# Decoder block on one core: the recurrent branch's output projection as seven block products under the attention, with its operands, weights and block differences prepared in other places

## The chip, the cores and the metric

The kernel runs on 1 core of a Trainium2 chip. The metric is the device time of one execution in microseconds (us). A TensorE (PE) matmul writes PSUM, a memory of eight banks of 128 x 512 fp32; VectorE (DVE), ScalarE (ACT) and GpSimd (POOL) work element by element, and SyncE (SP) issues most of the DMA transfers. Each engine works through its own queue in order.

## The reference

```python
h = rms_norm(x, g_norm) * (1 + scale) + shift            # x: 2048 x 1024
x_rnn, z_rnn, q, k, v, z_attn, g_r, g_a = split(h @ w_in)
xc = causal_depthwise_conv(x_rnn, conv_w, conv_b)
hr = rg_lru(xc, ...)                                      # a scan over the positions
y_rnn = (hr * silu(z_rnn)) @ w_out_rnn                    # 1024 x 1024: what the change touches
o = dilated_attention_mixture(rope(q), rope(k), v)
y_attn = (o * silu(z_attn)) @ w_out_attn
merged = sigmoid(g_r + b_r) * y_rnn + sigmoid(g_a + b_a) * y_attn
out = rms_norm(x + gate * (merged @ w_o), g_final)
```

## The kernel before

Every product is made in near-fp32: an operand is split into a high part and a low part (high = the value rounded to the matmul's format, low = the rest), and `mm3` (L154) issues three matmuls, high x high, high x low, low x high. What is called a product below is 12 such matmuls: a 128 x 512 block of weights against a 512 x 512 block of data, which fills one PSUM bank.

The kernel has three stages. In the **first**, run twice (f = 0, 1, one half of the 2048 positions each), `h @ w_in` is made by `strassen` (L355): two 128-column tiles of weights are a pair, and a pair is done in 7 products in place of 8, by block sums of both operands. A half has 28 pairs, that is 196 products. The order is written out by hand: `recurrent` (L928) is one pair per row tile m of the recurrent branch, followed by `others[m]` pairs of the other columns (others = 1, 2, 2, 1, 2, 2, 1, 3), so that the tiles m of a half start at products 0, 14, 35, 56, 70, 91, 112 and 126. Convolution, gates and scan of tile m are steps at fixed numbers of products after its pair (`steps_after`, L236), and the branch's result goes to a DRAM tensor `yaT`. In the second half the split weight sums of the first half come back from DRAM (`sD`, a ring of seven tiles S0 to S6, L319), one transfer of 512 KB per product. There, too, `output_weights` (L428) prepares the weights of the later projections: every 4 products a 128 x 512 half tile is loaded, split (ACT the high part, POOL the low part) and stored to `wD` in two transfers by ACT's queue; those of the attention's projection are stored unsplit to `wR` as well.

In the **second** stage the attention runs: 16 heads' halves of 6 units each, one unit per slot. In a slot PE makes scores, turns probabilities (`pT`) and sums values; DVE and ACT do the softmax and split the turned probabilities. Between these pieces lies the *fill*: `spend` (L1862) takes `FILL` steps per slot from the generator `steps` (L1731), 2.85 per slot in the first half of the heads and 2.75 in the second. A step is one `mm3` of 512 columns. The steps are those of the two output projections, in tiles of 8 steps (1024 rows of weights against 512 positions); a tile fills one PSUM bank, of which the pool `pj` has two here, and DVE multiplies it by the gate (`evict`, L1792), one step after the next tile's start. Under the attention lie `TAIL0` = 40 tiles: the recurrent branch's 32 (4 blocks of positions by 8 row tiles) and the attention's first 8. Weights come from `wD` one half tile at a time into a ring of four (L342), asked for three half tiles ahead; data tiles of `yaT` are split into high and low parts on DVE, ACT and POOL (L1771).

The **third** stage is the rest of the attention's projection and `w_o`.

Of the kernel before, what the change touches and what calls it, by code (L numbers as in the profile page):

```python
# [20 lines left out]
P = 128  # L21
# [13 lines left out]
FILL = (2.85, 2.75)  # L35
# [55 lines left out]
def decoder_block(ctx, tc, x, c, positions, g_norm, w_mod, b_mod, w_in, b_gate, conv_w, conv_b,  # L91
# [31 lines left out]
    wD = scratch("wD", [2, KT, 2, P, 2, KH, P])  # L123
# [195 lines left out]
    def load_next():  # L319
# [6 lines left out]
        elif n >= 28 * 7:  # L326
# [3 lines left out]
            if k < 3:  # L330
                load_wd(0, 0, k) if k < 2 else load_wd(0, 1, 0)
            if k == 1:

                t = T(hp, [P, KH, CH], F32, "T", bufs=14)
                nc.sync.dma_start(t[:], yaT[KH * P :, :CH].rearrange("(k p) j -> p k j", p=P))
                for i in range(KH):
                    Y0[True, 0, KH + i] = t[:, i, :]
# [4 lines left out]
    def load_wd(i, m, half):  # L342
        x = n_w[0]
        n_w[0] += 1
        W[x] = t = T(pS, [P, 2, KH, P], F32R, f"S{x % 4}")
        nc.sync.dma_start(t[:].bitcast(F32), wD[i, m, half])
# [81 lines left out]
    def output_weights():  # L428

        parts = [(i, w, m, half) for i, w in enumerate((w_out_rnn, w_out_attn)) for m in range(KT) for half in range(2)]  # L430
        for x, (i, w, m, half) in enumerate(parts):
            v = {}

            def load(v=v, w=w, m=m, half=half):
                v["raw"] = raw_tile([P, KH, P])
                rows = slice(half * KH * P, (half + 1) * KH * P)
                nc.sync.dma_start(v["raw"][:], w[0, rows, m * P : (m + 1) * P].rearrange("(k p) m -> p k m", p=P))

            def split(v=v):
                v["h"] = T(wq, [P, KH, P], F32R, "s1", bufs=1)  # L440
                v["l"] = T(wq, [P, KH, P], F32R, "s2", bufs=1)
                hi_act(v["h"][:], v["raw"][:])
                lo_pool(v["l"][:], v["raw"][:], v["h"][:])

            def store(v=v, i=i, m=m, half=half):
                for l, n in enumerate("hl"):
                    nc.scalar.dma_start(wD[i, m, half, :, l], v[n][:].bitcast(F32))
# [4 lines left out]
            for d, fn in ((1, load), (3, store_raw), (4, split), (5, store)) if i else ((1, load), (4, split), (5, store)):  # L452
                after_prod.setdefault(n_prod[0] + 4 * x + d, []).append(fn)
# [586 lines left out]

    def rotary_tables(rp, f):
# [287 lines left out]
    for f in range(2):  # L1329
# [21 lines left out]
        for m in range(KT):  # L1351
            recurrent(rp, bigr, f, m)
# [36 lines left out]
    NY = 9  # L1389
# [337 lines left out]
    TAIL0 = KT * (NB + 1)  # L1727
    RAW = 2 * TAIL0 + 1


# [501 lines left out]
```

## Time and profile before

| | |
|---|---|
| median of 3 runs | 2160.72 us (2160.36 to 2161.0) |
| the profiled execution's own time | 2161.23 us |
| its span, first to last instruction | 2159.4 us, granted clock 0.998 |
| first stage, second half (about 800 to 1340) | PE without a gap between 800 and 1200 |
| second stage (about 1345 to 1870) | PE busy 519.34 of 525 us, DVE 380.96, ACT 401.49, POOL 311.36 |
| third stage (2000 to 2160) | PE busy 151.63 of 160 us, DVE 121.95, ACT 57.96, POOL 83.27 |

A group's row gives busy time and the mean ns of one instruction. Matmul records overlap: one of 512 columns is shown with about 390 ns, but they follow each other more closely, so their cost is read from how many a stretch holds.

### The profile page before, as it was taken

The numbers are of one execution on the slowest core, as the hardware profiler recorded it, in microseconds if no ns is written. First come the engines' busy times: TensorE is split into PE (matmuls) and PEld (weight loads), VectorE is DVE, ScalarE is ACT, GpSimd is POOL, SyncE is SP. The second block draws the span as 40 slices with busy tenths as digits, with TensorE's granted clock in tenths as the row PEclk, the third lists the DMA queues.
The fourth block names the chain that finished last, engine by engine and source line by source line (L and its number), as shares of the span: only waits on it lengthen the run. The fifth ranks groups of instructions, "written<-read, shape, count | busy, mean of one in ns | idle before, by whom it ended". The sixth has DMA issues, their size and how long they took to land.

```text
span 2159.4 us, 32571 instructions
## 1 busy us (share of the span) xinstructions
PE 2136.6 (99%) x10539; PEld 1788.3 (83%) x10539; DVE 1463.3 (68%) x2582; ACT 1296.2 (60%) x2592; POOL 1120.6 (52%) x868
## 2 busy tenths in 40 slices
PE   9999999999999999999999999999999999999998
PEld 6888778888888888888888887889898988878887
DVE  6759878768656715544436684587777687788777
ACT  5748668668644527457457532677788888443333
POOL 1467667777666423223223675466666664432555
PEclk9999999999999999999999999999999999999999
DMA  8467887887655368899997676888887777899543
GB/s 301 142 211 256 280 290 264 288 294 244 174 115 166 108 229 291 301 305 311 323 318 240 152 173 171 300 269 263 273 275 218 256 236 239 300 316 300 181 170 114
DMA packets 416575, 521.39 MB, mean 241 GB/s; under 512 B 107574, under 2 KB 282898, under 8 KB 415380
## 3 DMA queue, kind: packets, MB, share of 16 engines
q1 hardware_dynamic: 376388, 401.65, 59.7%
q10 hardware_dynamic: 34384, 99.78, 12.2%
q0 software_dynamic: 5632, 17.88, 2.6%
q8 instruction: 83, 1.36, 0.3%
q14 instruction: 88, 0.72, 0.1%
HBM read 332.02 MB, written 187.17 MB: 240 GB/s over the span
## 4 chain that ended last, share of the span: by engine, by line
PE 71%; DVE 4%; DMA 3%; issue 1%; POOL 1%; ACT 1%; SPq 0%; ACTq 0%; POOLq 0%; DVEq 0%
PE X L152 14%; PE V L152 13%; PE pj L152 12%; PE Z L152 7%; PE W L152 7%; PE Y L152 6%; PE sc L152 4%; PE o L152 4%; PE pg L152 1%; PE pT L1568 1%; PE pT L1581 1%; DMA fg<-gaT 1%; DMA kraw<-kqT 1%; DVE ptl L169 1%; DVE yl L169 1%
## 5 line engine op out<-in xcount | busy, mean ns | idle before, releaser
L166 POOL TENSOR_TENSOR S<-R,S 128x512 fp32r<-128x512 f32 x192 | 295.3, 1546 | 169.3 <-ACT S L160 82.9
L152 PE MATMUL V<-T,S 128*128 128x512 f32 x1344 | 324.3, 390 | 1.9 <-DVE ev L461 1.9
L152 PE MATMUL X<-T,S 128*128 128x512 f32 x1344 | 323.8, 390 | 1.6 <-ACT u L391 1.3
L152 PE MATMUL pj<-yh,S 128*128 128x512 f32 x896 | 321.6, 402 | 1.3 <-DVE fg L1795 0.8
L152 PEld LDWEIGHTS X<-T,S 128*128 128x128 f32 x1344 | 251.8, 188 | 56.5 <-ACT u L391 2.9
L152 PEld LDWEIGHTS V<-T,S 128*128 128x128 f32 x1344 | 251.9, 188 | 55.9 <-issue 1.9
L166 POOL TENSOR_TENSOR S<-s,S 128x512 fp32r<-128x512 f32 x116 | 173.3, 1494 | 150.1 <-ACT S L160 114.3
L152 PEld LDWEIGHTS pj<-yh,S 128*128 128x128 f32 x896 | 168.3, 188 | 32.3 <-DVE S L169 1.3
L1481 ACT ACTIVATE pp<-pp,st 128x256 f32<-128x256 f32 (+3 forms) x256 | 133.8, 524 | 78.0 <-DVE st L1480 77.4
L152 PE MATMUL pj<-yl,S 128*128 128x512 f32 x448 | 175.5, 392 | 1.0 <-POOL yl L166 1.0
L160 ACT ACTIVATE S<-s 128x512 fp32r<-128x512 f32 x124 | 77.3, 624 | 145.1 <-DVE s L291 92.1
L152 PE MATMUL W<-T,S 128*128 128x512 f32 x672 | 161.6, 389 | 0.0
L152 PE MATMUL Y<-T,S 128*128 128x512 f32 x672 | 161.6, 389 | 0.0
L152 PE MATMUL Z<-T,S 128*128 128x512 f32 x672 | 161.4, 389 | 0.0
L160 ACT ACTIVATE S<-R 128x512 fp32r<-128x512 f32 x200 | 121.5, 622 | 59.0 <-DMA R<-in_w_in_dram 14.8
L169 DVE TENSOR_TENSOR ptl<-pT,pth 128x384 fp32r<-128x384 f32 (+1 forms) x160 | 97.8, 628 | 80.5 <-ACT pth L160 78.4
L152 PEld LDWEIGHTS W<-T,S 128*128 128x128 f32 x672 | 126.0, 188 | 26.9 <-issue 0.9
L152 PEld LDWEIGHTS Z<-T,S 128*128 128x128 f32 x672 | 126.2, 188 | 26.2
L152 PEld LDWEIGHTS Y<-T,S 128*128 128x128 f32 x672 | 126.1, 188 | 26.1
L166 POOL TENSOR_TENSOR s<-R,s 128x512 fp32r<-128x512 f32 x32 | 43.2, 1350 | 188.8 <-ACT s L160 164.6
L980 DVE SCALAR_TENSOR_TENSOR xc<-xr,par,xc 128x512 f32<-128x512 f32 x96 | 102.0, 1062 | 52.1 <-ACT xc L974 49.9
L1548 ACT ACTIVATE pp<-pp,M 128x256 f32<-128x256 f32 (+3 forms) x256 | 118.0, 523 | 12.8 <-DVE M L1680 12.8
(419 smaller groups left out, 4906.0 us busy)
## 6 DMA issues: line engine op xcount, KB each, us to landing
sD<-S ACTq DMA_DIRECT2D x140, 512.0 KB, 3.7
S<-sD SPq DMA_DIRECT2D x140, 512.0 KB, 5.0
S<-wD SPq DMA_DIRECT2D x82, 512.0 KB, 5.5
R<-in_w_in_dram SPq DMA_DIRECT2D x144, 256.0 KB, 3.3
wD<-s ACTq DMA_DIRECT2D x64, 256.0 KB, 5.1
kraw<-kqT SPq DMA_DIRECT2D x32, 384.0 KB, 5.1
T<-in_w_mod_dram SPq DMA_DIRECT2D x16, 512.0 KB, 9.1
vN<-ev SPq DMA_DIRECT2D x32, 256.0 KB, 2.7
```

What stands on the lines that cost most here:

```text
L152: nc.tensor.matmul(o, lhsT=l, rhs=r, start=st, stop=sp, **kw)
L160: nc.scalar.activation(o, i, AF.Copy)
L166: nc.gpsimd.tensor_tensor(o, i, h.bitcast(F32), ALU.subtract)
L169: return nc.vector.tensor_tensor(o, i, h.bitcast(F32), ALU.subtract).ins
L980: nc.vector.scalar_tensor_tensor(xc, xr[:, i : i + CH], cw(i), xc, ALU.mult, ALU.add)
L1481: nc.scalar.activation(pdst, pdst, AF.Exp, bias=m_, scale=-1.0, accum_out=l_)
L1548: nc.scalar.activation(pp, pp, AF.Copy, scale=w)
L1568: nc.tensor.transpose(pt[:, c0 + j * P : c0 + (j + 1) * P], pp[i][:, k * P : (k + 1) * P], ident)
L1581: nc.tensor.transpose(pt[:, c * P : (c + 1) * P], pp[:, half * P : (half + 1) * P], ident)
```

## The change

The recurrent branch's projection is cut into 2 x 2 blocks of 512: for each of two pairs of position blocks (q) and each of four pairs of row tiles (p), seven products give what eight gave, as the first stage does. Seven kinds of data block (`BLOCKS`: two parts of `yaT` as B11, B21, then the sums T2, T3, T1, T4, and B22) times two q are the 14 groups g of the new loop; in a group the same four data tiles serve four products, one per p. A product is 4 steps in one bank of `pj` in place of 8, so the fill has 224 steps for this projection where it had 256, and `FILL` is 2.54 and 2.44. The pool `pj` still has two banks.

What goes with it:
- Weights: `output_weights` loads four quarter blocks per p, makes four sums on DVE and splits and stores seven tiles (`wB`), one every 3 products; the attention's half tiles follow every 3 products in place of 4, four of them between p = 1 and p = 2.
- Data sums: `block_sums` loads four 128 x 512 tiles of `yaT`, makes four differences on POOL and stores them to `tB`, all issued by SP. Six of its eight calls run in the second half of the first stage, in the buffers of the recurrence (gi, y, a, t or xc, xh, xl) between two of its uses, at products 24 to 30 after the start of m = 1, 2, 4 and 5 and at 19 to 25 after that of m = 5 and 7; two run at the start of the attention.
- In the fill, data tiles are loaded straight into one of eight pairs of operand tiles (F0 to F13 and S3) during the first steps of the group before, and split there: high part on ACT for half of the first seven groups and on DVE otherwise, low part on POOL. Weights have a ring of three tiles and are asked for two tiles ahead.
- Eviction (`block_evict`): a copy (B11), one addition (T2, T3), two operations (B21, T4, B22) or three (T1).

The core of the diff:

```diff
-FILL = (2.85, 2.75)
+FILL = (2.54, 2.44)
...
+    def load_w_tile(src, ring=4):
...
+    BLOCKS = (("B11", 0), ("B21", 4), ("T2", 1), ("T3", 2), ("T1", 3), ("T4", 5), ("B22", 6))
+    N_WB = 2 * 7 * KH
+
+    def load_wb(x):
+        load_w_tile(wB[BLOCKS[x // KH % 7][1], x % KH], 3)
...
     def output_weights():
...
+        n0, PITCH = n_prod[0], 3
...
+            on_n(n, split)
+            on_n(n + 1, store)
...
+            for x, (i, name, *sums) in enumerate((
+                (5, "a22"), (3, "a22", "a21", "a22", ALU.add), (0, "a11"), (1, "a22", "a22", "a11", ALU.subtract),
+                (2, "a21", "a11", "a21", ALU.subtract), (4, "a12"), (6, "a12", "a12", "a22", ALU.subtract))):
...
+    def block_sums(q, k, on_step, tiles):
...
+        def combine(dst, a, b):
+            nc.gpsimd.tensor_tensor(raws[dst].bitcast(F32), raws[a].bitcast(F32), raws[b].bitcast(F32), ALU.subtract)
+
+        def store(i, src):
+            nc.sync.dma_start(tB[q, i, k], raws[src].bitcast(F32))
+
+        for d, fn, *args in ((0, load, *B11), (0, load, *B12), (0, load, *B22), (1, load, *B21),
+                             (3, combine, B11, B12, B11), (3, combine, B12, B22, B12), (4, combine, B22, B22, B11),
+                             (4, store, 0, B11), (4, store, 2, B12), (5, combine, B21, B21, B22), (5, store, 1, B22),
+                             (6, store, 3, B21)):
...
-    TAIL0 = KT * (NB + 1)
+    NT = 1
+    TAIL0 = KT * NT
...
+        def block_evict(g, p, ps):
+            name = BLOCKS[g % 7][0]
+            tt = nc.vector.tensor_tensor
+            if name == "B11":
+                U[p] = T(fl, [P, CH], F32, f"F{14 + p}")
+                nc.vector.tensor_copy(U[p][:], ps[:])
+            elif name in ("T2", "T1"):
+                tt(U[p][:], ps[:], U[p][:], ALU.add)
+            elif name == "T3":
+                Q[p] = T(pR, [P, CH], F32, f"R{p}")
+                tt(Q[p][:], ps[:], U[p][:], ALU.add)
+            if name in OUT:
+                t = G[g, p]
+                tt(ps[:], ps[:], (Q if OUT[name][0] else U)[p][:], ALU.add)
+                tt(t[:], ps[:], t[:], ALU.mult)
...
+        for g in range(14):
+            for p in range(KH):
+                ps = T(pj, [P, CH], F32, "pj")
+                x = KH * g + p
+                for k in range(KH):
+                    j, n = KH * p + k, KH * (g + 1)
+                    if k == 1:
+                        if x:
+                            (load_wb(x + 2) if x + 2 < N_WB else load_w(x + 2 - N_WB))
...
+                        if last:
+                            block_evict(*last)
...
+                    w, (yh, yl) = W[x], OT[KH * g + k]
+                    mm3(ps[:], w[:, 0, k, :], w[:, 1, k, :], yh[:], yl[:], first=k == 0, last=k == KH - 1)
...
+                    if j < KH and n + j > 6:
+                        operand(n + j)
+                    if j >= 8 and j % 2 == 0 and n + j // 2 - 4 > 6:
+                        split(n + j // 2 - 4)
```

The change also alters what stands where. DVE's queue at the start of the attention, before: kq are the first head's queries and keys (L169 makes their low parts, which wait for a load and for ACT), pj the fill's banks, sc the scores, pp the softmax.

```order
L169 TENSOR_TENSOR kq_2215_12040<-kraw_2235_12086,kq_2215_12040 128x512
L169 TENSOR_TENSOR kq_2215_12040<-kraw_2236_12088,kq_2215_12040 128x512
L1795 TENSOR_TENSOR fg_2232_12073<-pj_2233_12077,fg_2232_12073 128x512
L169 TENSOR_TENSOR kq_2215_12040<-kraw_2238_12092,kq_2215_12040 128x512
L1442 CAST q1_2244_12148<-kq_2215_12040 128x512 x2
L1480 ISA pp_2247_12159,st_2245_12151<-sc_2246_12152,msk_2214_12038 128x128
L1480 ISA st_2245_12151 128x1
L1480 ISA pp_2247_12159,st_2245_12151<-sc_2246_12152,msk_2214_12038 128x256
L1480 ISA st_2245_12151 128x1
L1795 TENSOR_TENSOR fg_2242_12133<-pj_2240_12118,fg_2242_12133 128x512
```

The same place now (F14 to F17 are the sums U of the four p):

```order
L1934 COPY F14_2286_12284<-pj_2278_12255 128x512
L171 TENSOR_TENSOR kq_2263_12224<-kraw_2279_12262,kq_2263_12224 128x512
L171 TENSOR_TENSOR kq_2263_12224<-kraw_2280_12264,kq_2263_12224 128x512
L1934 COPY F15_2289_12305<-pj_2284_12278 128x512
L171 TENSOR_TENSOR kq_2263_12224<-kraw_2282_12268,kq_2263_12224 128x512
L1516 CAST q1_2291_12322<-kq_2263_12224 128x512 x2
L1554 ISA pp_2294_12333,st_2292_12325<-sc_2293_12326,msk_2262_12222 128x128
L1554 ISA st_2292_12325 128x1
L1554 ISA pp_2294_12333,st_2292_12325<-sc_2293_12326,msk_2262_12222 128x256
L1554 ISA st_2292_12325 128x1
L1934 COPY F16_2297_12344<-pj_2287_12299 128x512
L1911 TENSOR_REDUCE S3_2283_12276<-S3_2283_12276 128x512
```

Four steps fill a bank now, so between the same pieces of the attention stand three evictions in place of two; the second and the third still come behind the low parts of kq.

SP's queue in the second half of the first stage, around product 112, before (each S<-sD is one product's weights; ev and zs are results on their way out):

```order
L324 DMA S6_1850_9988<-sD 128x1024
L324 DMA S0_1851_9990<-sD 128x1024
L437 DMA R3_1852_9995<-in_w_out_attn_dram 128x4x128
L324 DMA S1_1855_10012<-sD 128x1024
L1188 DMA kqT<-ev_1846_9951 384x1x128
L1188 DMA kqT<-ev_1846_9951 128x1x128
L324 DMA S2_1859_10036<-sD 128x1024
```

The same place now:

```order
L326 DMA S6_1880_10105<-sD 128x1024
L326 DMA S0_1881_10107<-sD 128x1024
L1091 DMA tB<-xc_1864_10012 128x512
L1091 DMA tB<-xc_1865_10014 128x512
L326 DMA S1_1886_10132<-sD 128x1024
L1260 DMA kqT<-ev_1877_10067 384x1x128
L1260 DMA kqT<-ev_1877_10067 128x1x128
L1085 DMA gi_1887_10141<-yaT 128x512
L1085 DMA y_1888_10143<-yaT 128x512
L1085 DMA a_1889_10145<-yaT 128x512
L1091 DMA tB<-xh_1866_10016 128x512
L326 DMA S2_1893_10166<-sD 128x1024
```

Between the same weights SP now issues three stores of differences, which wait for POOL, and three loads of the next call.

204 lines of the change are left out of this document (155 added, 49 removed).

## Prediction

> **What bounds the kernel now.** I read first the busy shares on the page, then the table of stretches, then the chain and the waits, and last the timeline at the start of the attention. From the page:
>
> ```profile
> span 2159.4 us, 32571 instructions
> PE 2136.6 (99%) x10539; PEld 1788.3 (83%) x10539; DVE 1463.3 (68%) x2582; ACT 1296.2 (60%) x2592; POOL 1120.6 (52%) x868
> PE 71%; DVE 4%; DMA 3%; issue 1%; POOL 1%; ACT 1%; SPq 0%; ACTq 0%; POOLq 0%; DVEq 0%
> ```
>
> PE is idle for 23 us in all, and the chain is mostly PE. So time is won by issuing fewer matmuls, and lost wherever PE is made to wait. Three stretches (columns: PE, PEld, DVE, ACT and POOL busy, granted clock, DMA share, GB/s): within the first stage's second half, the part of it that gets the most new transfers, and the attention:
>
> ```profile
> 800.00:1000.00 200.00, 200.00 (x883) 165.32 (x882) 101.18 (x144) 115.81 (x179) 56.39 (x44) 1.00 0.89 300
> 1063.00:1136.00 73.00, 73.00 (x324) 60.32 (x323) 28.94 (x37) 35.66 (x55) 23.32 (x18) 1.00 0.96 323
> 1345.00:1870.00 525.00, 519.34 (x3359) 464.56 (x3358) 380.96 (x1100) 401.49 (x1114) 311.36 (x269) 1.00 0.82 259
> ```
>
> The first row prices a matmul: 883 of 512 columns in 200 us without a gap are 0.2265 us each (their own records, about 0.39 us, overlap). A product of 12 is 2.72 us, a step of three 0.68 us. PE never waits in the first two rows although the DMA engines are 0.89 and 0.96 busy. In the attention DVE is idle for 144 of 525 us.
>
> **What is removed.** The fill has 32 steps fewer: 96 matmuls x 0.2265 = 21.7 us, all on PE and so all on the path. This is the only gain; the first and third stages keep their matmuls.
>
> **DVE, ACT and POOL in the attention.** The groups there:
>
> ```profile
> L1795 DVE TENSOR_TENSOR fg<-pj,fg 128x512 f32<-128x512 f32 x40 | 27.3, 683 | 0.5 <-PE pj L152 0.5
> L1777 DVE TENSOR_REDUCE yh<-R 128x512 fp32r<-128x512 f32 x32 | 21.5, 677 | 0.0
> L169 DVE TENSOR_TENSOR yl<-R,yh 128x512 fp32r<-128x512 f32 x18 | 17.3, 967 | 0.6
> L166 POOL TENSOR_TENSOR yl<-R,yh 128x512 fp32r<-128x512 f32 x19 | 25.0, 1316 | 19.1 <-DMA vraw<-vN 5.6 <-DVE yh L1777 4.4 <-PE sc L152 3.2
> L169 DVE TENSOR_TENSOR ptl<-pT,pth 128x384 fp32r<-128x384 f32 (+1 forms) x160 | 97.8, 628 | 80.5 <-ACT pth L160 78.4
> ```
>
> Evictions: B11 and T2 and T3 take one DVE operation each, B21, T4 and B22 two, T1 three, 12 for each of the 8 pairs of q and p: 96 where there were 32, so 64 more x 0.683 = 43.7 us. High parts on DVE: 47 where there were 32, 15 x 0.677 = 10.2 us. Low parts on DVE: 6 where there were 18, 12 x 0.967 = 11.6 us less. DVE goes from 381 to 423 us while the stretch shrinks from 525 to 503: 84% in place of 73%. POOL gets 37 more low parts at 1.316 and 8 differences at the same price: 59 us, from 311 to 370, 74%. ACT gets ten high parts, about 6 us. None of the three is full; each costs something only where PE waits for its next result.
>
> **Where PE will wait: the banks.** A tile was 8 steps, is now 4, and `pj` still has two banks. The eviction is put one step into the next tile, and the bank is wanted again when that tile ends: three steps later in place of seven. Two places of the timeline, PE and DVE, show how much of that there is:
>
> ```profile
> 1497.36 0.39 PE L152 MATMUL pj<-yh,S 128*128 128x512 f32 x1
> 1500.44 0.69 DVE L1795 TENSOR_TENSOR fg<-pj,fg 128x512 f32<-128x512 f32 x1
> 1504.01 0.40 PE L152 MATMUL pj<-yh,S 128*128 128x512 f32 x1
> ...
> 1409.85 0.62 PE L152 MATMUL pj<-yh,S 128*128 128x512 f32 x2
> 1415.65 0.68 DVE L1795 TENSOR_TENSOR fg<-pj,fg 128x512 f32<-128x512 f32 x1
> 1416.52 0.48 PE L152 MATMUL pj<-yh,S 128*128 128x512 f32 x1
> ```
>
> In each triple the first row ends a tile, the second is its eviction, and the third lies where the bank would be wanted under the new count (at the first place one step, 0.7 us, before that). The first bank would be free 3.6 us early, the second 0.2 us. A second eviction operation takes 0.68 us of that, and DVE's other new work (42 us over 111 slots) another 0.4; against that a slot has fewer steps, so three steps last about 0.4 us longer. So a tile like the first stays hidden and one like the second makes PE wait about 0.5 us. Of 56 tiles, none waiting costs 0 and half waiting 28 x 0.5 = 14 us; I take 3 us, nearer the first, since PE's waits before were all short.
>
> **Where PE will wait: the start of the attention.** Rows of PE, DVE and ACT:
>
> ```profile
> 1340.43 0.39 PE L152 MATMUL pj<-yh,S 128*128 128x512 f32 x1
> 1350.89 0.84 PE L152 MATMUL sc<-kq 128*128 128x128 f32 x5 [0.40 <-DVE kq L169]
> 1349.48 0.63 ACT L160 ACTIVATE kq<-kraw 128x512 fp32r<-128x512 f32 x1 [9.47 <-DMA kraw<-kqT]
> 1350.14 0.69 DVE L169 TENSOR_TENSOR kq<-kraw,kq 128x512 fp32r<-128x512 f32 x1 [5.79 <-ACT kq L160]
> 1352.57 0.69 DVE L169 TENSOR_TENSOR kq<-kraw,kq 128x512 fp32r<-128x512 f32 x1 [1.74 <-ACT kq L160]
> 1353.18 0.68 DVE L1795 TENSOR_TENSOR fg<-pj,fg 128x512 f32<-128x512 f32 x1
> 1355.89 0.69 DVE L169 TENSOR_TENSOR kq<-kraw,kq 128x512 fp32r<-128x512 f32 x1 [2.03 <-ACT kq L160]
> 1357.77 0.69 DVE L1795 TENSOR_TENSOR fg<-pj,fg 128x512 f32<-128x512 f32 x1
> ```
>
> The first scores need kq, which comes from DRAM at 1350.8 whatever the fill does. Before, 14 steps (9.5 us from 1340.43) covered that; with `FILL` at 2.54, 12 steps (8.2 us) do, and PE waits from 1348.6, 2.2 us. The scores last to 1351.5. The fourth tile then needs the second tile's bank, whose copy stands behind the second kq operation: 1353.3 plus 0.7 is 1354.0, so 2.4 us more. It ends at 1356.7, and the fifth needs the third tile's bank, whose copy stands behind the third kq operation and the first softmax, where now the row at 1357.77 is: it is done at 1358.5, 1.8 us. Together 6.4 us, less the 1.2 that PE waits here now (0.4 for kq and 0.8 for fg), and another 1 us while the next slots work off DVE's queue, where B21's evictions are two operations: I take 6 us. The lower bound is 0 (kq earlier, or the order of readiness kinder); the upper 10, since weights are asked for 7 steps ahead, 4.8 us in this dense part, against 5.5 us to landing (row below), which may hold each of the first tiles for a little more.
>
> ```profile
> S<-wD SPq DMA_DIRECT2D x82, 512.0 KB, 5.5
> q1 hardware_dynamic: 53737, 93.18, 74.4%
> q10 hardware_dynamic: 11511, 20.96, 15.1%
> ```
>
> The last two rows are the queues of SP and ACT from 800 to 1180. Later in the attention 7 steps last some 12 us, so weights are there in time.
>
> **Where PE may wait: transfers in the first stage.** Weights: 24 more stores of 256 KB, and 3 products per half tile in place of 4. Block sums: six calls of eight 256 KB transfers. Three calls fall between products 94 and 121, which is 1063 to 1136 with the half's start at 1340.4 less 196 x 2.72. In those 73 us the engines are busy for 0.96 x 73 = 70 us now. Added are 3 x 2.1 = 6.3 MB, and 2.4 MB of weights (9 half tiles of 1.05 MB in place of 6.75); the two queues move 330 and 365 MB per ms of engine time (93.18 MB in 74.4% of 380 us, 20.96 in 15.1%), so 8.7 MB are 25 us. That makes 95 us of transfers in 73, 22 too many. The view of transfers for this stretch, with its rate in 40 slices:
>
> ```profile
> GB/s 347 377 282 347 389 394 339 224 272 237 302 288 315 259 361 384 370 404 382 303 364 130 285 375 285 301 360 385 358 361 279 361 336 331 146 296 226 370 400 398
> S<-sD SPq DMA_DIRECT2D x26, 512.0 KB, 5.6
> ```
>
> PE does not feel a surplus at once: weights come back from DRAM seven products, 19 us, before their use and land in 5.6, so 13 us are in hand. By that PE would lose 9 us. But the landing is no longer here, at a share of 0.96, than under the attention at 0.82 (5.5), and slices reach 404 GB/s: at some 400 the 32.3 MB (323 GB/s x 73 us are 23.6 now, and 8.7) would take 81 us, 8 too many, and the 13 in hand would hold them. Bounds: 0 and 22; I take 2, nearer the slices. DVE's 16 sums, ACT's 12 and POOL's 12 more splits and POOL's 24 differences lie in a stage where POOL is 28% and DVE half busy, beside a PE that waits for neither: nothing. Queued behind a store that waits for POOL are SP's weight loads; that is part of the same 13 us.
>
> The Trainium skill, HBM Reference, section Specifications (TRN2), gives about 358 GB/s per core when both cores of a pair stream; by that figure the stretch would take 90 us, 17 too many, and PE would lose 4 us in place of my 2, an estimate. One core runs here, and 17 of the slices are above that figure, so the trace does not bear it out.
>
> **The sum.** 2161.2 (profiled execution) - 21.7 + 6 + 3 + 2 = 2150.5 us; the median lies 0.5 below the profiled execution: 2150 us. With all costs at their lower ends 2139, with all at the upper ones 2160.7 - 21.7 + 46 = 2185.
>
> **The rivals.**
> - Everything hides: DVE has idle time enough, and the start finds its data. 2139 us. For it: PE waited for `fg` only once, 0.8 us. Against: the start's waits are read off the order and the times of kq. Chance 0.13.
> - The transfers of the first stage do fill the engines: 22 us too many less the 13 in hand, 9 in place of 2, 2157 us; with the stores to `tB` eating half of what is in hand, 2163. For it: 0.96 in the row. Against: landings that have not grown, and the slices. Chance 0.10.
> - The banks bind: half of the tiles wait, 14 in place of 3, 2161 us, and nothing is won. For it: the place at 1415.65. Against: DVE catches up whenever PE waits. Chance 0.11.
> - Slower: DVE becomes the bound of the attention. Its 144 idle us are mostly waits for ACT in the middle of its queue (78.4 in the ptl row). If these stay as they are, 423 + 144 = 567 us in place of 525, and 2203. The point from which it decides: the attention may last 503 us without loss, so DVE must give up 64 of the 144; keeping over 106 of them makes the kernel slower than before. Against: these waits shrink by themselves when DVE runs late, since ACT is then done. Chance 0.08.
>
> **How the numbers follow.** My forecast, 2145 to 2156, has 0.58. A measurement of this kernel can tell about 0.2%, 4.3 us, from no change. Faster by more (below 2156.4): 0.58 + 0.13 = 0.71. Within it: the transfers' 0.10 and the banks' 0.11, 0.21. Slower: 0.08. Range: 2139, where everything hides, to 2162, which takes in the banks' case and the nearer half of the transfers'; what is left out is the slower rival and the costs' joint upper ends.
>
> **What would show it.** Right: the attention's stretch about 513 us where it is 525, with some 6 us of PE waits between 1345 and 1362 for kq and for pj's copies; small waits of pj for L1942 to L1943; DVE near 423 us; no PE gap, or one or two, between 1060 and 1170. Wrong: waits of X, V or W for S<-sD or for `ev` in the first stage over 5 us; waits of PE for DVE in the attention over 15 us; or an attention near 503.

## The result and the profile after the change

| | before | after | difference |
|---|---|---|---|
| median (4 runs each) | 2160.54 us | 2209.59 us | ratio 1.0229, 95% interval 1.0211 to 1.0247 |
| the profiled execution's span | 2159.4 us | 2207.6 us | +48.2 |
| first matmul of the fill (`pj`), the attention's beginning | 1340.4 us | 1370.4 us | +30.0 |
| from there to the last sum of values (`o`) | 522.3 us | 538.7 us | +16.4 |
| from there to the last matmul | 288.9 us | 290.8 us | +1.9 |

The change makes the kernel 2.3% slower, where I had forecast 0.5% faster. The attention has 21.7 us of matmuls less and is 16.4 us longer, so about 38 us of delay came in there, and 30 in the first stage: 68 in all. The page of the changed kernel, its span, its engines and its chain:

```profile
span 2207.6 us, 32849 instructions
PE 2141.1 (97%) x10442; PEld 1778.1 (81%) x10443; DVE 1532.3 (69%) x2664; ACT 1304.2 (59%) x2613; POOL 1223.7 (55%) x949
PE 24%; DMA 6%; DVE 6%; POOL 2%; issue 2%; ACT 2%; SPq 1%; ACTq 0%; POOLq 0%; DVEq 0%
```

PE has 97 matmuls fewer and is idle for 66 us where it was for 23. The chain can be followed back only to 1221 us here and to 393 before, so its shares add up to 43% and 81% of the span; PE has 24 of the 43 where it had 71 of the 81, and transfers, DVE and POOL have more of it. Stretches of the changed kernel (columns as in the prediction): the first stage's second half, three parts of it, and the attention.

```profile
800.00:1370.40 570.40, 550.60 (x2373) 448.10 (x2372) 322.99 (x396) 298.73 (x470) 265.67 (x190) 0.99 0.86 277
1063.00:1136.00 73.00, 66.45 (x277) 53.00 (x276) 27.64 (x32) 32.62 (x51) 30.77 (x23) 0.95 1.00 343
1100.00:1160.00 60.00, 51.80 (x206) 40.79 (x206) 21.50 (x25) 22.53 (x38) 26.28 (x20) 0.91 1.02 352
1370.40:1909.10 538.70, 508.10 (x3245) 447.63 (x3244) 417.46 (x1160) 401.54 (x1117) 361.49 (x312) 0.98 0.82 263
```

The same of the kernel before, where the first row was 540.40 us without any idle time:

```profile
1100.00:1160.00 60.00, 60.00 (x266) 49.62 (x265) 25.62 (x31) 31.64 (x51) 15.74 (x12) 1.00 0.94 315
1340.40:1862.70 522.30, 516.64 (x3347) 462.27 (x3346) 377.96 (x1096) 398.32 (x1109) 309.51 (x268) 1.00 0.82 259
```

In the first stage the transfer engines went from 0.94 to 1.02 busy around 1100 to 1160, and PE does 206 matmuls there in place of 266. In the attention DVE, ACT and POOL are as busy as forecast (417, 402 and 361 us; I had 423, about 407 and 370). PE's idle time is 19.8 us in the first row and 30.6 in the last (5.7 before), 45 us more in all; the other 23 of the 68 passed while PE counted as busy, and the granted clock in these rows is below 1. PE's waits, first stage from 800 on, then attention:

```profile
PE V L154 <- DVE ev L496: 9.3, 3, 4.0
PE pg L154 <- POOL xl L168: 6.5, 4, 3.5
PE X L154 <- ACT u L400: 2.7, 3, 1.9
...
PE sc L154 <- POOL q L1516: 6.3, 5, 2.9
PE pj L154 <- DMA S<-wB: 6.1, 3, 4.6
PE pj L154 <- POOL F L168: 5.7, 3, 2.2
PE pj L154 <- DVE F L1934: 3.4, 2, 2.7
PE sc L154 <- ACT sm L1710: 2.7, 4, 1.2
```

No wait names `S<-sD`, the weights for which I had counted the time in hand, and none of any size the evictions of two operations, L1942 and L1943; L1934, the copy of B11, is named twice, both times in the attention's start.

Two measures serve below, each worked out from the traces. **First stage:** the 196 products' begin times of the second half against those of the kernel before give the delay gathered by a product. **Attention:** for a given one of its 2400 matmuls for scores, turning and sums, the time since the attention's beginning, less the same of the kernel before, plus 0.2265 us for each fill matmul that has been issued fewer; what stands there at the 144th (about 60 us in) I call the start, what comes on top until the last the rest. For the changed kernel the start is 69.7 - 57.7 + 18 x 0.2265 = 16.1 us and the whole 16.5 + 102 x 0.2265 = 39.6, so the rest is 23.5. What a run had lost or won ahead of the half's first product (-0.9 to 3.6 us), and behind its last one (1.5 to 3.3, in e6, e8 and e9), is not in the table.

| delay, us | up to product 70 | 70 to 112 | 112 to 140 | 140 to 154 | 154 to 196 | attention: start | rest |
|---|---|---|---|---|---|---|---|
| after the change | 7.1 | 1.5 | 15.2 | 7.1 | 0 | 16.1 | 23.5 |
| no sums (e1) | 1.1 | 0 | 0 | 0 | 0 | 5.5 | 23.9 |
| copies, one operation (e2) | 5.4 | 3.0 | 21.4 | 1.7 | 0 | 16.4 | 11.2 |
| no differences, lows on DVE (e3) | 11.1 | 0 | 16.6 | 1.7 | 0 | 13.5 | 31.6 |
| stores by POOL (e4) | 9.5 | 0.5 | 15.1 | 8.4 | 0 | 12.5 | 23.2 |
| no wR, gates on POOL (e5) | 5.5 | 0 | 9.9 | 6.0 | 0 | 18.7 | 27.8 |
| late calls, no odd lows (e6) | 3.6 | 0 | 0 | 0.7 | 16.7 | 19.3 | 13.9 |
| no sums, one operation (e7) | 1.2 | 0 | 0 | 0.3 | 0 | 4.7 | 11.5 |
| late calls, all of it (e8) | 3.8 | 0 | 0 | 0.5 | 16.5 | 25.6 | 27.6 |
| late calls on DVE, highs on ACT (e9) | 4.7 | 0 | 0 | 1.2 | 10.8 | 23.2 | 23.4 |
| no sums, one operation, no odd lows (e11) | 1.9 | 0 | 0 | 1.7 | 0 | 6.1 | 3.5 |

In the changed kernel most of the first stage's delay falls in a call of `block_sums` or in the products just behind it: m = 2's is at products 59 to 65, m = 4's at 94 to 100, m = 5's two at 110 to 121, m = 7's at 145 to 151. Only m = 1's, at 38 to 44, costs nothing.

### The profile page after: what moved, and what is told of

Same layout as the page of the kernel before. It is cut to its first block, busy times and chain, and to the rows that moved or that the text cites. A ratio compares the mean times of both kernels' runs of the same rounds, so it can differ in the third digit from the quotient of the medians.

```text
span 2207.6 us, 32849 instructions
## 1 busy us (share of the span) xinstructions
PE 2141.1 (97%) x10442; PEld 1778.1 (81%) x10443; DVE 1532.3 (69%) x2664; ACT 1304.2 (59%) x2613; POOL 1223.7 (55%) x949
## 2 busy tenths in 40 slices
DMA packets 431570, 546.59 MB, mean 248 GB/s; under 512 B 109254, under 2 KB 284578, under 8 KB 430372
## 3 DMA queue, kind: packets, MB, share of 16 engines
HBM read 342.50 MB, written 201.85 MB: 247 GB/s over the span
## 5 line engine op out<-in xcount | busy, mean ns | idle before, releaser
L154 PE MATMUL V<-T,S 128*128 128x512 f32 x1344 | 330.7, 396 | 10.2 <-DVE ev L496 10.2
L154 PE MATMUL pj<-F,S 128*128 128x512 f32 x1164 | 310.4, 402 | 15.4 <-DMA S<-wB 6.1
L154 PEld LDWEIGHTS V<-T,S 128*128 128x128 f32 x1344 | 255.9, 191 | 67.3 <-DVE ev L496 10.8
L154 PEld LDWEIGHTS pj<-F,S 128*128 128x128 f32 x1164 | 209.8, 190 | 56.4 <-POOL F L168 6.8
L168 POOL TENSOR_TENSOR s<-R,s 128x512 fp32r<-128x512 f32 x44 | 57.7, 1311 | 195.7 <-ACT s L162 73.2
L162 ACT ACTIVATE S<-R 128x512 fp32r<-128x512 f32 x200 | 121.5, 622 | 59.0 <-DMA R<-in_w_in_dram 15.2
L1554 DVE CUSTOM_DVE_ANT_0 pp<-sc,msk 128x256 f32<-128x256 f32 (+3 forms) x256 | 103.3, 448 | 19.4 <-PE sc L154 18.6
```

The costliest lines, as they stand in the source:

```text
L154: nc.tensor.matmul(o, lhsT=l, rhs=r, start=st, stop=sp, **kw)
L162: nc.scalar.activation(o, i, AF.Copy)
L168: nc.gpsimd.tensor_tensor(o, i, h.bitcast(F32), ALU.subtract)
L1554: nc.vector.tensor_tensor_reduce(pdst, s_ps, mask, 1.0, 3e38, ALU.add, ALU.min, m_)
```

## The experiments

My first theory (A in the expectations) was that the calls hold the queues: SP's loads and stores wait for the recurrence's buffers and for POOL, and all that stands behind them is late. Rivals: B, the weights prepared at a pace of three products; C, DVE's evictions, for the attention; D, the bytes themselves. Each kernel was run once, with a profile, beside the kernel before; the effects are read inside the trace, by stage. The same first stage in e1, e7 and e11 began the attention at 1341.9, 1345.5 and 1343.4, which shows how far one such time can be trusted.

**The calls left out (e1).**

```diff
-            if f:
-                block_sums_behind(rp, m)
...
-                    src = (tB[q, int(name[1]) - 1, k] if name[0] == "T" else
-                           yaT[(i * KH + k) * P : (i * KH + k + 1) * P, (2 * q + j) * CH : (2 * q + j + 1) * CH])
+                    src = (yaT[(i * KH + k) * P : (i * KH + k + 1) * P, (2 * q + j) * CH : (2 * q + j + 1) * CH])
```

> All eight calls of block_sums are left out; the fill's T operands are loaded from unsummed blocks of yaT in place of tB, so its loads and matmuls are as many as after the change. In the changed kernel the attention begins at 1370.4 us where it began at 1340.4 before, and lasts 538.7 us to the last sum of values. Theory A (the calls hold the queues in order: SP's loads and stores wait for the recurrence's buffers and for POOL's differences, and what stands behind them is late): the attention begins at 1340 to 1344, and its first 60 us, where two calls lie, lose 8 to 12 us less, so it lasts 526 to 531; the whole about 2168. Rival B (the weights, prepared every three products in place of four with 24 more stores, are what delays): the beginning stays above 1360. Rival C (DVE's evictions in the attention): the beginning falls but the attention stays at 536 or more.

Measured: the attention begins at 1341.9 and lasts 528.6; the whole takes 2171.1 us. B falls. The calls cost 28.5 of the first stage's 30 us and 10 us of the attention, all of these in its start. The row of this kernel where the double call would be:

```profile
1100.00:1160.00 60.00, 60.00 (x266) 49.62 (x265) 25.46 (x31) 32.86 (x51) 18.51 (x14) 1.00 1.00 352
```

The transfer engines are already full here, with the new weights alone, and PE does not wait: the weights took up all the room there was.

**The same bytes without buffers or sums (e2); one eviction operation fewer.**

```diff
+            if (q, k) not in ((1, 2), (1, 3)):
+                nc.sync.dma_start(tB[q, 2 * half + j, k], yaT[(half * KH + k) * P : (half * KH + k + 1) * P, n * CH : (n + 1) * CH])
+                return
             raws[half, j] = t = tiles[half, j]()
...
-                tt(ps[:], ps[:], (Q if OUT[name][0] else U)[p][:], ALU.add)
                 tt(t[:], ps[:], t[:], ALU.mult)
```

> First stage: each of the six calls becomes eight transfers of 256 KB from yaT straight to tB, issued by SP at the same places, with no buffer, no wait for POOL and no differences: the same bytes written, the queue never held by a buffer. Theory A: the attention begins at 1340 to 1347. Rival D (the bytes fill the transfer engines): it begins at 1360 to 1372. Attention: the evictions lose their addition of U or Q for the output kinds (32 operations of 0.68 us on DVE, 22 us, left out). Theory A with POOL as the engine that is late there: the attention stays at 534 to 539. Rival C (DVE's evictions hold the two banks): it falls to about 520.

Measured: the attention begins at 1372.8. For most of the first stage theory A has little left and D holds, with one exception: at m = 7, where the transfer engines have room, the copies lose 1.7 us where the calls lost 7.1. That part is either the buffers or the differences, both of which are missing here; the next run tells them apart. The copies go from DRAM to DRAM: the engines move as many bytes as in the changed kernel (546.57 MB against 546.59), but DRAM is read 6.3 MB more and written 6.3 MB more (348.79 and 208.15 MB against 342.50 and 201.85). So the 24.4 us lost from product 70 to 140, against 16.7, are no measure of the calls' own transfers. The attention lasts 526.7, between what C and A said; its rest falls from 23.5 to 11.2, so DVE's evictions matter, and they are not all. The waits of pj for F and for wB stay as they were (6.1 and 6.0 us).

**POOL's differences left out; half of the operands' low parts on DVE (e3).**

```diff
         def combine(dst, a, b):
-            nc.gpsimd.tensor_tensor(raws[dst].bitcast(F32), raws[a].bitcast(F32), raws[b].bitcast(F32), ALU.subtract)
+            if (q, k) in ((1, 2), (1, 3)):
+                nc.gpsimd.tensor_tensor(raws[dst].bitcast(F32), raws[a].bitcast(F32), raws[b].bitcast(F32), ALU.subtract)
...
-                (lo_dve if raw is not None and n > 4 else lo_pool)(l[:], src, h[:])
+                (lo_dve if n % 2 or raw is not None and n > 4 else lo_pool)(l[:], src, h[:])
```

> First stage: the six calls keep their loads and stores in the recurrence's buffers, but the 24 differences on POOL are left out. If POOL's differences (24 x 1.3 us, and the stores that wait for them) are what holds SP, the attention begins at 1340 to 1350; if the buffers are (the loads wait for the recurrence to give them up, and the recurrence waits for the stores to land), it stays at 1360 or more. Attention: half of the operands' low parts (those of odd number, about 26) go from POOL (1.3 us each) to DVE (0.97). If POOL's queue is what is late, the waits of pj for F by POOL and of sc for q by POOL (13 us together) fall to under 5 and the attention lasts 526 to 533; if DVE is the tight engine, it lasts 540 or more.

Measured: it begins at 1369.9, so in sum the differences hold nothing up. By place they do: at m = 7 the loss falls from 7.1 to 1.7 us, as in e2, although the loads, the stores and the buffers stay; with no call at all e11 loses 1.7 there too. So that part is POOL's differences and not the buffers. The trace of the changed kernel shows how; its rows of POOL, DVE and PE there:

```profile
1242.75 1.75 POOL L1088 TENSOR_TENSOR xl<-xl,xh 128x512 f32<-128x512 f32 x1
1244.46 1.28 POOL L168 TENSOR_TENSOR S<-s,S 128x512 fp32r<-128x512 f32 x1
1245.77 1.74 DVE L293 TENSOR_TENSOR s<-s,R 128x512 f32<-128x512 f32 x1 [2.43 <-POOL S L168]
1248.63 0.68 DVE L496 TENSOR_TENSOR ev<-V,u 128x512 f32<-128x512 f32 x1
1249.37 4.60 PE L154 MATMUL V<-T,S 128*128 128x512 f32 x12 [3.93 <-DVE ev L496]
```

The low part S of a weight sum stands behind the last difference on POOL, DVE waits for S, `ev` stands behind that on DVE, and PE waits for `ev`. At m = 2 the loss up to product 70 is 11.1 us where it was 7.1, which hides this in the sum; over the five runs with the calls in their old places it lies between 5.4 and 11.1, and what moves it was not tried.

The attention lasts 544.4: with 27 us off POOL and 21 more on DVE its rest grows by 8.

**The stores issued by POOL (e4).**

```diff
-            nc.sync.dma_start(tB[q, i, k], raws[src].bitcast(F32))
+            nc.gpsimd.dma_start(tB[q, i, k], raws[src].bitcast(F32))
```

> The stores to tB, in the first stage and in the attention, are issued by POOL behind its own differences, so that SP no longer waits for POOL at them; loads, buffers and differences stay. If the stores are what holds SP, most of the 30 us come back: the attention begins at 1345 to 1355, and the start of the attention loses 4 us less. If the loads' wait for the buffers holds it, it stays at 1360 to 1372.

Measured: 1373.0, so SP's wait at the stores is not it either. In the attention the start falls from 16.1 to 12.5, the 4 us expected: there, a store that waits for POOL does hold back the loads behind it on SP.

**4.2 MB taken away elsewhere, the calls kept (e5); half of the gates on POOL.**

```diff
-            on_n(b + 4, store_raw)
...
-                nc.sync.dma_start(t[:, 1].bitcast(F32), wR[m, x % 2])
+                nc.sync.dma_start(t[:, 1].bitcast(F32), wD[m, x % 2][:, 0])
...
+                u = (Q if OUT[name][0] else U)[p]
+                if name in ("T4", "B22"):
+                    tt(u[:], ps[:], u[:], ALU.add)
+                    nc.gpsimd.tensor_tensor(t[:], u[:], t[:], ALU.mult)
```

> First stage: the 16 stores of the attention's raw half tiles (256 KB each, 4.2 MB, between products 46 and 137) are left out, and the third stage reads the stored high parts in their place; the calls of block_sums stay. Theory D (the transfer engines are full until about product 137, before the change already nearly, and the loss is what is added): 4.2 MB at 350 GB/s are up to 12 us, so the attention begins at 1358 to 1364 in place of 1370. If bytes are not the cause it stays at 1368 to 1373. Attention: for T4 and B22 the multiplication by the gate (16 x 0.68 us on DVE, 11 us) goes to POOL (about 1.3 us each, 21 us). Theory C (DVE's evictions hold PE): 532 to 536 in place of 538.7. Theory A (POOL is late): 540 or more.

Measured: it begins at 1361.3, 9.1 us earlier, inside what D expected. The attention lasts 545.7, as A would have it and not C: with 20 us more, POOL keeps PE waiting for `q`:

```profile
PE sc L154 <- POOL q L1515: 12.4, 8, 2.9
```

**Five calls moved to where the transfer engines have room (e6); the odd low parts left out.**

```diff
-    NS, NRAW = 7, 5
+    NS, NRAW = 6, 5
...
-            block_sums(0, (1, 2, 4, 5).index(m), on_step(24), tiles(("gi", 1), ("y", 2), ("a", 1), ("t", 1)))
-        if m in (5, 7):
+            if m == 1:
+                block_sums(0, (1, 2, 4, 5).index(m), on_step(24), tiles(("gi", 1), ("y", 2), ("a", 1), ("t", 1)))
...
+            for x, (q, k) in enumerate([(0, 1), (0, 2), (0, 3), (1, 0), (1, 1)]):
+                block_sums(q, k, lambda d, fn, x=x: after_prod.setdefault(n_prod[0] + 1 + 8 * x + d, []).append(fn),
...
-                (lo_dve if raw is not None and n > 4 else lo_pool)(l[:], src, h[:])
+                if raw is not None or n % 2 == 0:
+                    (lo_dve if raw is not None and n > 4 else lo_pool)(l[:], src, h[:])
```

> First stage: of the six calls the one behind m = 1 stays, the other five are moved to products 155 to 193, where the transfer engines are 0.2 to 0.9 busy, eight products apart, in buffers of their own (the ring of stored weight sums has six tiles in place of seven and the residual gate's weights one buffer in place of two, for room). Theory D: the attention begins at 1341 to 1347. If a call costs PE time wherever it lies (SP's queue held by its waits), it begins at 1360 or more. Attention, with its two calls: the operands' odd low parts are left out (about 26 operations of 1.3 us, 34 us of POOL), nothing goes to DVE for it. Theory A (POOL is late): 526 to 532. Theory C (DVE): 536 to 540, as after the change.

Measured: 1366.8, a miss, though D is right about the old place: between products 70 and 150, where the changed kernel lost 17 us, nothing is lost. The loss has moved. 3.6 us come before product 70, at products 59 to 62. What differs from e1 up to there is m = 1's call, some 15 products earlier, and the smaller ring of stored weights; two of the waits, 1.9 us, are for `S<-sD`, which fits the ring. 16.7 come behind product 154, where the rebuilt weight sums need POOL and DVE; the longest single wait, 4.4 us, is for the residual gate (`gacc`), whose steps the edit moved too. The stretch, and PE's waits in it:

```profile
1230.00:1366.80 136.80, 122.63 (x510) 94.91 (x508) 83.85 (x94) 33.13 (x59) 101.11 (x68) 0.97 0.76 201
```

```profile
PE pg L154 <- DVE gacc L1345: 4.4, 1, 4.4
...
PE V L154 <- DVE t L496: 2.1, 4, 0.7
PE V L154 <- ACT S L162: 1.7, 2, 1.0
PE X L154 <- POOL S L168: 1.2, 2, 0.8
```

The transfer engines are 0.76 busy and POOL is busy for 101 of 137 us. The attention lasts 532.4, and its rest is 13.9 in place of 23.5: 27 us off POOL with nothing given to DVE save 9.6. So the odd lows are a cause beside the additions, and A and C are both right about the rest. By which way is not settled: DVE is busy 8 us less here too (409.6 in place of 417.5), because some of its smallest operations no longer last as long as POOL's (the last section has the rows).

**Calls and additions left out together (e7).** The edits of e1 and of e2's attention.

> All eight calls are left out (T operands are loaded unsummed from yaT) and the 32 output evictions lose their addition on DVE (22 us). The attention lasts 528.6 us without the calls and 526.7 without the additions, 538.7 with both. If the two are separate causes, the savings add: 515 to 518. If both only relieve the same wait (the first 60 us, or SP's queue), 523 to 528. What is over 500.6 (522.3 less the 21.7 us of matmuls) is then neither's. The attention begins at 1341 to 1343.

Measured: 515.5. The savings add, so they are two causes: the calls in the start, the additions in the rest.

**All of the work, with the calls late (e8).** The edits of e6 without its last, with the gates of e5 and POOL's stores of e4 in the attention's two calls.

> Computes all of it. The five calls late as in the run before (theory D: the attention begins at 1341 to 1347), T4's and B22's gates on POOL, and the stores of the attention's two calls issued by POOL behind its differences (3.8 us less when all stores were). By theory C the attention lasts 529 to 533; the whole is then 2168 to 2178 us, 32 to 42 less than after the change and still 8 to 17 over the kernel before.

Measured: 2221.4 us, slower than the change itself, a miss. It begins at 1366.3 as e6 does, and the attention lasts 552.4: late calls run into the start (25.6), and the gates on POOL make the rest 27.6, as in e5.

**Late calls with their differences on DVE (e9); high parts on ACT.**

```diff
-            nc.gpsimd.tensor_tensor(raws[dst].bitcast(F32), raws[a].bitcast(F32), raws[b].bitcast(F32), ALU.subtract)
+            (nc.gpsimd if (q, k) in ((0, 0), (1, 2), (1, 3)) else nc.vector).tensor_tensor(raws[dst].bitcast(F32), raws[a].bitcast(F32), raws[b].bitcast(F32), ALU.subtract)
...
-                if raw is not None or n % 2 == 0 and n < 7 * KH:
+                if raw is not None or n % 4 < 3:
                     hi_act(h[:], src)
```

> Computes all of it. The five calls at products 155 to 193 again, but their differences on DVE in place of POOL, and the residual gate's last two steps a few products later: the run with late calls lost 5.7 us up to product 70 and 17 more behind product 150, 4.4 of it in one wait for the residual gate and the rest in waits for POOL's and DVE's parts of the rebuilt weight sums. If POOL was what those late calls held up, the second part falls to 2 to 5 us and the attention begins at 1349 to 1354; if any extra work there is too much, it stays at 1360 or more. Attention: three of four operand high parts on ACT (about 22 operations of 0.68 us, 15 us, off DVE). By theory C that saves 5 to 9 us: 530 to 534 in place of 538.7; if ACT's queue is as tight as the other two, 537 or more.

Measured: it begins at 1360.6; the part behind product 154 is 10.8, less than 16.7 and more than the 2 to 5 expected if POOL alone were in the way. The attention lasts 545.8, a miss; its rest is 23.4, as if nothing had been moved, though 16 us went from DVE to ACT. The whole takes 2206.1 us.

**All three left out (e11).** The edits of e1, of e2's attention and of e6's odd lows.

> All calls, the 32 additions of the output evictions and the odd low parts of the operands (34 us of POOL) are left out. The attention lasted 515.5 us without the first two; leaving the odd lows out alone took 6.3 us off it. If POOL's lateness is a cause beside DVE's, 508 to 511 us; if it only mattered because DVE was late too, 513 to 516. 500.6 would be no wait at all.

Measured: 508.7, the rest is 3.5. With e7 and e6 this closes the attention's sum: 10.6 us are the calls, 12 the additions, 8 to 10 the odd low parts, and of 39.6 there remain 9.6, of which 6.1 lie in the start.

**Deliberate pauses in the kernel before (e10), and the small tile alone (e12).**

```diff
+    pz = T(cp, [P, 8], F32, "pz")
...
+        mm(ps[:1, :8], ones[:, 0:1], pz[:], True, True)
+        nc.vector.tensor_copy(pz[:1, :], ps[:1, :8])
+        for _ in range(n):
+            nc.vector.tensor_scalar(pz[:], pz[:], 1.0, None, ALU.mult)
+        ps = T(pg, [P, CH], F32, "pg")
+        mm(ps[:1, :8], ones[:, 0:1], pz[:], True, True)
```

> The kernel before, with eight deliberate pauses of PE in the first stage's first half, behind products 10, 25, 46, 60, 81, 105, 120 and 137 of that half: PE makes a tiny matmul, DVE copies its result and works off a chain of 4 to 50 tiny operations, and PE's next matmul needs the last of them. In the traces so far PE's pauses of over about 2.1 us are followed by 3.4 us at a granted clock of 0.5 and those under 2.0 are not. If the pause itself does that, the long ones here are each followed by such a spell, and cost about 1.7 us more than they last; if the spells come from something else in the changed kernel (its DMA load, say), none appears here.

Measured: each of the eight pauses (3.75 to 14.45 us, 63.5 in all; DVE's other work made them longer than its chains) brings on a spell of 3.4 to 13.7 us at a granted clock of 0.5, which begins before the pause ends, and PE loses some 2 to 3 us more at each than the pause lasts. One of them on the timeline, and then the stretch of its spell and the one behind:

```profile
159.31 0.20 PE L152 MATMUL pg<-pz,ones 128*1 128x8 f32 x2 [3.75 <-DVE pz L923]
159.44 4.48 PE L152 MATMUL V<-T,S 128*128 128x512 f32 x12
163.75 2.96 PE L152 MATMUL X<-T,S 128*128 128x512 f32 x12
```

```profile
159.20:162.60 3.40, 3.29 (x10) 2.58 (x11) 2.58 (x5) 1.64 (x4) 1.19 (x1) 0.50 0.47 170
163.00:173.00 10.00, 10.00 (x44) 8.03 (x44) 7.69 (x10) 8.23 (x13) 4.02 (x5) 1.00 0.61 202
```

So the pause does it, not the change's transfers. The limit of about 2.1 us for a single pause does not hold as such; the last section says what does. The whole takes 2274.6 us, 113 more than before, of which the pauses and their spells are 85. The rest lies in the products, which take 2.80 us from the first one on.

> The kernel before with the run of pauses' small tile (32 bytes per partition, behind which other tiles of the pool and of later pools have other addresses) and no pause. In the run of pauses every product of the first stage took 2.80 us in place of 2.72, from the first on and ahead of the first pause. If the tile's place does that, the products take 2.80 us here too, and the whole is about 392 x 0.08 = 31 us longer than before, 2190 to 2195. If the pauses did it, products take 2.72 and the time is 2159 to 2164.

Measured: 2191.6 us, 32 more than before, and products at 2.80 us: the tile does that, not the pauses. The changed kernel's products take 2.72, so this is no part of its loss.

## Why the prediction was wrong, point by point

- **What is removed, 21.7 us.** This term holds by its arithmetic; it was not tried alone. With the calls, the additions and half of the low parts left out (e11), the whole was 2152.3 us, 9 less than the kernel before beside it (2161.7).
- **Transfers in the first stage, +2: measured 30, the largest error.** The working already had what is needed: 25 us of new transfers in a stretch 0.96 full. It failed in three steps. I counted three of the six calls: m = 2's and m = 7's, 7 us each, are not in the sum. I took peaks of the forty slices, 404 GB/s, for a rate that could be kept: over 73 and 60 us the full engines carried 343 and 352. And the 13 us in hand were those of `sD` alone: its loads landed 7.4 us after their issue (5.8 in e1, 5.5 before), so they stayed in hand, and they helped none of the transfers that PE did wait for. With the weights alone the engines are at 1.00 (e1), so what came on top had to be paid in full: three calls of 2.1 MB at 352 GB/s are 18 us, and products 94 to 140 lost 16.7. At m = 7, where the engines have room, 5.4 of the 7.1 us are POOL's differences (e3), which I had put at nothing because POOL was 28% busy. The Trainium skill's figure, HBM Reference, Specifications (TRN2), is about 358 GB/s per core beside a streaming neighbour; I set it aside because single slices lie above it, and the full stretches agree with it, though no neighbour streams here; the 425 that the page gives for a core alone they do not reach. By the 358 I had 4 us, since I took the 13 in hand off there as well.
- **"That is part of the same 13 us."** What ran late was never `sD`. It was DVE's `ev`, POOL's `xl` and ACT's `u`. Between 1095 and 1170 us DVE's `ev` waits 12.5 us for stores of earlier `ev` (kqT, grT) to land and ACT's `u` 5.9 for a store to `tB`; in m = 2's call `xl` stands behind POOL's differences, the first of which waits 7.7 us for its load; at m = 7 it is POOL's queue (e3). None of these has a ring of seven behind it. I named this sign (waits for `ev` over 5 us) as one that would prove me wrong; it is 9.3.
- **The start, +6: measured 5.5 (e1) for what the term priced.** The size is right, in part by luck: PE waits 4.0 us for the copies in e1 (2.4 and 1.8 in the working), but 0.2 for kq in place of 2.2, and the 3.4 us at half clock behind the longer wait, up to 1.7 us, were not in the term. And the two calls that lie there were counted as 8 operations of POOL and nothing else; they cost 10.6, of which SP's waits at the stores are 3.6 (e4) and the others were not taken apart.
- **The banks, +3: the mechanism did not show.** Behind the start PE hardly ever waits for a bank. The same additions cost 12 us otherwise.
- **"None of the three is full; each costs something only where PE waits for its next result."** The loads were forecast well (417, 402, 361 us), and the price of nothing was the error: 23.5 us. My reading is that PE's chain runs through all three engines at every unit, so that an operation put ahead in a queue is late work for all that hangs on it, at 75% busy too; single operations were not followed to show it. Taking 21 us from DVE gave back 12 (e2), 27 from POOL gave 10 (e6); moving work among the three gave back nothing (e9) or cost 4 to 8 us (e5, e3).
- **A term that was missing: the clock.** The changed kernel has eight spells at half clock from 800 us to the end of the attention, 34 us in all, the kernel before one of 3.4. The pause at POOL's `xl` in m = 2's call, and the product behind it beside the one that follows, with the stretches of the spell and after it:

```profile
975.16 0.50 PE L154 MATMUL pg<-xl,gh 128*128 128x512 f32 x1 [3.54 <-POOL xl L168]
...
976.44 4.50 PE L154 MATMUL V<-T,S 128*128 128x512 f32 x12
980.77 2.88 PE L154 MATMUL X<-T,S 128*128 128x512 f32 x12
```

```profile
976.50:979.90 3.40, 3.40 (x10) 2.63 (x9) 1.09 (x2) 1.12 (x2) 1.57 (x2) 0.50 1.06 416
982.00:992.00 10.00, 10.00 (x46) 8.28 (x45) 6.50 (x9) 8.43 (x14) 2.75 (x3) 1.00 0.96 384
```

  The product takes 4.50 in place of 2.88 us, 1.6 more. Ten such stretches of 3.4 us are up to 16 of the 23 us that passed while PE counted as busy; what the others are stays open.
- **The rivals.** The transfers' rival (2157 or 2163) had the right mechanism for most of the first stage, with a loss of 9 us, or 15 with the stores, where 30 came. The slower rival (DVE becomes the bound of the attention, 2203) came near the time by another way: DVE kept 121 us of idle time in an attention of 538.7, but POOL's low parts have nearly as large a share in the rest's loss as DVE's additions, and 30 of the 68 us of delay came in the first stage.

No kernel tried beats the one before with all of the work in it. Of the places that the calls were given, only m = 1's was free. Elsewhere something else was in the way: the transfer engines before product 140, POOL's queue at m = 7, POOL and DVE behind product 154, and in the attention, for a part, SP's waits for POOL.

## What to carry to other kernels

When several edits draw on one resource, price them together, at the rate that full stretches keep. Time in hand belongs to the one queue that it was worked out for; once the engines are full, the others pay for every byte. A change that takes 22 us of matmuls off PE and adds 95 us to three engines that PE's chain runs through has to find room in their queues, not in their busy shares. And a pause of PE of some 2 us or more can cost up to 1.7 us on top, for each 3.4 us at half clock that it brings on.

## What the runs showed of the hardware

- **Half clock after a pause.** In each trace here the clock changes only at multiples of 3.41 us from one another, so time falls into windows of that length. What counts is PE's idle time within a window, by its records. Over all 14 traces, without the first and last 30 us, no window at full clock with under 1.5 us idle (4213 of them) is followed by one at half clock, 14 of the 33 with 1.5 to 2.0 us are, and all 65 with 2.0 us or more are. So a pause of 2.87 us that fell across two windows brought on none (e9), and two of 1.1 and 1.2 us that left 2.1 us of one window idle did (the changed kernel, at 1150.6). The Trainium skill, TensorE: Matmul & The Clock Gate, Part 1, has the clock at half after at least one idle window of about 3.4 us, in windows that run freely. The length and the free running agree with the traces; that the window must be idle throughout does not: by that rule the pauses of 2.2 to 2.9 us that brought on three of the changed kernel's eight spells could not have done so.
- **A tiny DVE operation can last as long as POOL's.** The operation that begins the softmax's weights (M, 128 x 16) takes 0.17 us each time in the kernel before. In the changed kernel five of its sixteen take 0.75 to 2.96 us, and each of these five ends within 0.04 us of the end of a POOL instruction; with the odd low parts left out on POOL (e6) one is long. The rows of before, after and e6:

```profile
L1675 DVE TENSOR_TENSOR M<-dm,xs 128x16 f32<-128x16 f32 x16 | 2.7, 172 | 3.0 <-ACT dm L1671 3.0
L1749 DVE TENSOR_TENSOR M<-dm,xs 128x16 f32<-128x16 f32 x16 | 10.3, 644 | 2.4 <-ACT dm L1745 2.4
L1753 DVE TENSOR_TENSOR M<-dm,xs 128x16 f32<-128x16 f32 x16 | 4.0, 247 | 2.4 <-ACT dm L1749 2.4
```

- **A tile of 32 bytes per partition made every product of the first stage 3% slower.** In e12 a product takes 2.80 us in place of 2.72, with a granted clock of 0.999. The attention begins 26.1 us later (1366.5 against 1340.4), 3.9 more come behind it, and the whole takes 32 us more than the kernel before beside it. The new tile gives the tiles behind it other addresses; which of them matters, and by what alignment, was not tried.

```profile
654.80 2.96 PE L152 MATMUL X<-T,S 128*128 128x512 f32 x12
657.60 2.96 PE L152 MATMUL V<-T,S 128*128 128x512 f32 x12
660.40 2.96 PE L152 MATMUL Z<-T,S 128*128 128x512 f32 x12
```
